# Ten weight buffers of a transformer trunk divided in another way during attention and the output projection

## The chip, the core and the metric

The kernel runs on one core of a Trainium2 chip. A core has five engines that run side by side, each with an instruction queue of its own that is worked off in order: TensorE (PE in the profile; its weight loads are listed apart as PEld), VectorE (DVE), ScalarE (ACT), GpSimd (POOL) and SyncE (SP), which here only issues DMA transfers. They share an on-chip memory of 128 partitions; matrix products land in a second one, PSUM. Engines wait for each other through semaphores. The metric is the time of one execution on the device in microseconds (us); the median of three runs before the change is 2564.08 us.

## What is computed

The reference is a stack of two layers over 1040 positions (16 learned ones and 1024 of the input) of width 1024, in float32. Each layer has two halves, each added to the residual:

```python
xn = rms_norm(h, attn_norm[i])
gq, gk, gv, gr, glr, fq, fk, fv, ff = jnp.split(xn @ w_in[i], cuts, axis=-1)
log_a = jax.nn.log_sigmoid((glr @ w_alpha_up[i] + b_alpha[i])) / GLA_TAU
o_gla = gla_chunk_causal(gq * GLA_DK ** -0.5, gk, gv, log_a)       # 4 heads, chunks of 64
o_gla = rms_norm(o_gla, gla_norm[i]) * jax.nn.silu(gr)
log_f = jax.nn.log_sigmoid((ff + b_forget[i]))
o_fox = rms_norm(forgetting_attention(fq, fk, fv, log_f), fox_norm[i])   # 8 heads, softmax
h = h + jnp.concatenate([o_gla, o_fox], axis=-1) @ w_out[i]
h = h + conv_ffn(rms_norm(h, ffn_norm[i]), w_up[i], conv_w[i], conv_b[i], w_down[i])
```

GLA is a gated linear attention with a decaying state, FoX a softmax attention with a forget bias, and `conv_ffn` an up-projection, a causal convolution of width 3, a SiLU gate and a down-projection. A last norm follows the second layer.

## The kernel before

**Activations and weights.** Activations lie transposed: eight slabs k of 128 features by 1040 positions. A weight tile m is 128 output columns of a matrix, cut into eight blocks k of 128 by 128. To keep float32 accuracy each operand is split into a rounded value ("hi", type float32r) and the remainder ("lo"), and each product is three matmuls, hi by hi, lo by hi and hi by lo: lines 225, 226 and 227, in `mm3`.

**Preparing a weight tile** (`weights`, line 174). For each half of a tile (four blocks, 128 x 512 elements, 256 KB) there are three steps: SyncE issues a DMA into a landing buffer "raw" (line 183), ScalarE rounds raw into "hi" (line 192), and VectorE, or GpSimd while `att` is set and the tile isn't one of the output projection's, subtracts hi from raw into "lo" (line 194). The buffers come from the pool "w": four for raw, three for hi and three for lo, ten of 2 KB per partition. A buffer that is asked for again waits until all that read it before have finished: raw until the cast and the subtraction are through, hi and lo until TensorE has made the last matmul with them. Callers can also hand in buffers of their own (`slots`, `keep`), and then only raw comes from the pool.

**Attention of a layer** (`attention`). `head` (line 366) computes the first three tiles; its first one is rounded by `narrow_weights`, with two hi buffers of the pool, the others lie in buffers of their own. Then come the rest of GLA and FoX. The products of a tile are work items (`add_tile`, `unit`): a tile is multiplied chunk by chunk, with three chunks of positions, and all eight blocks in each. When a tile's first chunk starts, the weights of the next tile are asked for, so that at most the running and the next tile hold buffers. These items fill TensorE between the steps of FoX (`fox`): scores, softmax, transposes, products with the values.

After the last FoX head come the first NSPLIT = 4 tiles of the output projection, summed over seven of the eight blocks in the order KORD = 4, 5, 0, 1, 2, 3, 6 and fed by VectorE's and ScalarE's splits of the mixed heads ("mh", "ml"). The last steps of FoX run among them. In attention a scheduler, which sees the whole program and an estimate of each instruction's time, sets the order on every engine, by program order among what is ready.

**The rest of the output projection** (in `ffn_up`, function `wout`, "wo" in the profile) runs twice over the eight tiles, once for each half of the positions, in an order written out by hand (`orders`). Tiles 0 to 3 have only their eighth block left, tiles 4 to 7 all eight; tiles 5 and 6 keep their weights from the first pass in other buffers (`keep`). The next tile's weights are asked for before the running tile's matmuls are issued. In the second pass VectorE and ScalarE also build the FFN's norm and its first operands ("x"); "ssq" is a small matmul that sums squares for that norm, the second one of which follows the first FFN block.

**The FFN** takes hi, lo and raw from the same pool (`block_operand`, `up_split`, from line 1003 on; rounding in lines 1042 and 1043), every second operand from a pool of its own. Its first loads and operands are asked for in `wout` at the start of the very last tile (`ensure(0)`, line 1116), five operands ahead. From the output projection on the order of TensorE's instructions is the program's.

Of the kernel before, what the change touches and what calls it, by code (L numbers as in the profile page):

```python
# [57 lines left out]
class Slots:  # L58


    def __init__(self):
        self.free = []
        self.lent = []
# [27 lines left out]
        return self.t[i]  # L91


class PsumTags:
    def __init__(self, tags):
        self.tags = tags

    def tile(self, shape, dtype, tag, name):
        pool, tag, bufs = self.tags[tag]
        return pool.tile(shape, dtype, tag=tag, name=name, bufs=bufs)  # L100
# [36 lines left out]
class Kern:  # L137
    def __init__(self, ctx, tc, hT0, wm, wd, vec, wau, out):
# [14 lines left out]
        nc.vector.memset(self.ones[:], 1.0)  # L153
        self.eps = self.vec[:, V_FIN + KD:]
        nc.vector.memset(self.eps, EPS)
        self.wp = ctx.enter_context(tc.tile_pool(name="w", bufs=3))
        self.slots = Slots()
        self.slots.add(ctx.enter_context(tc.tile_pool(name="slots", bufs=1)), NSLOT, "s")
        dp = ctx.enter_context(tc.tile_pool(name="dr", bufs=1, space=DRAM))
# [723 lines left out]
    def attention(self, lyr, nm, hsrc, chunks, feed):  # L883
        tc, nc, s = self.tc, self.nc, self.slots
        with tc.tile_pool(name=f"aps{lyr}", bufs=2, space=PSUM, reuse_waits="tile") as pp2, \
# [5 lines left out]
            with tc.tile_pool(name=f"gla{lyr}", bufs=1, reuse_waits="tile") as gp:  # L891
# [27 lines left out]
                g = [{"rem": rem}, {"rem": rem}]  # L919
                tiles = [(self.wm[lyr, M_REM], ev_rem)] + self.gla_products(lyr, 0, gp, pp, nm, g[0])  # L920
                self.head(tiles[:3], pp, nm, fd)
                if fd:
                    fd["end"]()
                add(tiles[3:])
# [121 lines left out]
    def ffn_up(self, lyr, mix, hT, pp, fw, halves, o0, during_last):  # L1046
# [14 lines left out]
        def operand(x):  # L1061
            X[x] = [[s.get(F32R, f"x{x}", (128, 2, 520)) for _ in range(2)] for _ in range(2)]
# [22 lines left out]
        def ensure(i):  # L1085
            while len(ops) < min(i + AHEAD + 1, len(seq)):
                ops.append(self.up_operand(lyr, *seq[len(ops)], fw, raws, len(ops) % 2))
# [22 lines left out]
        def wout(i, h):  # L1110
            m = orders[h][i]
            k0 = KD - 1 if m < NSPLIT else 0

            def f(w):
                if h == 1 and i == KD - 1:
                    ensure(0)
                ps = bank2("wo", (0, 1, 2, 0, 1, 3, 2, 1)[i] if h else i % 4)
                for k in range(len(w)):
                    for c in range(2):
                        self.mm3(ps[:, c, :n], w[k], mix[k0 + k], halves[h] + c * n, n, k == 0, k == len(w) - 1)  # L1120
                x = hT[m][:, sl[h]]
                nc.vector.tensor_tensor(out=two(x), in0=used(ps), in1=two(x), op=ALU.add)
                nc.gpsimd.dma_start(self.hm[m][:, sl[h]], x)
                if i == 0:
                    nc.scalar.activation(acc[:, sl[h]], x, AF.Square)
                else:
                    t = half(sq, i % 2)
                    nc.scalar.activation(t, x, AF.Square)
                    nc.vector.tensor_tensor(out=acc[:, sl[h]], in0=acc[:, sl[h]], in1=t, op=ALU.add)
                if h == 0:  # L1130
                    return
                if m < NSPLIT:
                    nc.scalar.mul(half(gt, m % 2), x, gain(m))
                else:
                    nc.vector.scalar_tensor_tensor(out=diff(m - 4), in0=x, scalar=gain(m), in1=half(gt, m % 2),
                                                   op0=ALU.mult, op1=ALU.subtract)
                if i == 1:
                    scale(0)
                    operand(1)
                    operand(2)  # L1140
                for k in turn.get(i, ()):
                    first_operand(k)
            return f
# [13 lines left out]
        for this, nxt in zip(todo, todo[1:] + [None]):  # L1157
            w, ahead = ahead, nxt and wout_weights(*nxt)
# [97 lines left out]
        for i, (j, p) in enumerate(seq):  # L1256
# [7 lines left out]
            ps, w = q[bank], ops[i]  # L1264
# [452 lines left out]
```

## Time and profile before

| what | value |
| --- | --- |
| three runs | 2564.07, 2564.08 and 2564.76 us |
| profiled execution | 2572.09 us, its span from the first to the last instruction 2570.3 us |
| mean granted TensorE clock | 0.99 |
| matmuls | 19278 |
| weight loads by DMA of 256 KB from the matrices in and up | 330 from SyncE's queue, median 2.9 us from issue to landing |

The stages, in us from the start of the span:

| stage | layer 0 | layer 1 |
| --- | --- | --- |
| attention: head, GLA | 0 to 182 | 1286 to 1450 |
| FoX | 182 to 463 | 1450 to 1730 |
| end of FoX with the first four output tiles | 463 to 531 | 1730 to 1798 |
| output projection | 531 to 585 | 1798 to 1858 |
| FFN up | 585 to 1034 | 1858 to 2309 |
| FFN down | 1034 to 1286 | 2309 to 2570 |

The profile describes one execution. Its page lists the busy time of each engine, the busy shares in 40 slices, the DMA queues, the chain of work that ended last and the costliest groups of instructions. A row of a group reads: line, engine, operation, output <- inputs, shapes, count, then busy time and mean of one, then the idle time of its engine just ahead of it with what ended it. In an order of time a row starts with the time in the span and the duration, and a bracket at its end gives the idle time ahead of it and what released it. Rows of SPq are SyncE's DMA queue. A matmul's row is longer than its share of time, since matmuls overlap.

### The profile page before, as it was taken

The page shows a single profiled execution, that of the slowest core. Times are in us where ns is not written, and L with a number is a line of the kernel's source. Part 1 is how long each engine was busy: PE and PEld are TensorE (multiplying, and loading weights), DVE is VectorE, ACT ScalarE, POOL GpSimd, SP SyncE. Part 2 cuts the span into 40 slices and gives each one's busy share as a digit, 9 for nine tenths or more (in the row PEclk, how much of TensorE's full clock was granted, in tenths as well). Part 3 has the DMA queues.
Part 4 walks back from the last instruction along what each step waited for, and adds up shares of the span by engine and source line. Part 5 has one row for each costly group of instructions (what it writes and reads, how often), then busy time and mean ns, then how long its engine had stood idle before and what let it go on. Part 6 is the DMA issues. An engine that isn't in the chain of part 4 may idle for free.

```text
span 2570.3 us, 48489 instructions
## 1 busy us (share of the span) xinstructions
PE 2496.6 (97%) x19278; PEld 2428.1 (94%) x19278; DVE 1756.6 (68%) x3394; ACT 1271.3 (49%) x2577; POOL 407.8 (16%) x582
## 2 busy tenths in 40 slices
PE   8999999999999999999999999999999999999998
PEld 7989999898999999999999899998999999999997
DVE  7655676769877777753655665676697777687435
ACT  7346666546444445641443565664464444455312
POOL 4033333210000000100301233331100000001002
PEclk9999999999999999999999999999999999999999
DMA  3232134342322224763312232152423222257712
GB/s 128 67 86 73 41 96 129 104 145 82 116 77 81 79 75 141 194 181 89 106 51 67 73 90 83 39 164 90 149 78 104 75 86 76 80 165 176 200 52 72
DMA packets 118514, 260.90 MB, mean 102 GB/s; under 512 B 14880, under 2 KB 32544, under 8 KB 118288
## 3 DMA queue, kind: packets, MB, share of 16 engines
q1 hardware_dynamic: 93984, 182.79, 22.7%
q0 software_dynamic: 22432, 72.71, 10.3%
q8 instruction: 151, 2.47, 0.4%
q10 hardware_dynamic: 1872, 2.31, 0.3%
q14 instruction: 75, 0.61, 0.1%
HBM read 177.16 MB, written 67.81 MB: 95 GB/s over the span
## 4 chain that ended last, share of the span: by engine, by line
PE 50%; issue 30%; DVE 13%; DMA 3%; ACT 3%; POOL 1%; SPq 0%; DVEq 0%; POOLq 0%; ACTq 0%
PE mm L225 8%; PE mm L226 7%; PE mm L227 7%; PE down L225 5%; PE down L227 5%; PE down L226 5%; PE av L724 2%; PE tr L706 2%; DVE P L677 2%; DVE x L1067 1%; PE S L669 1%; PE wo L226 1%; PE wo L225 1%; PE wo L227 1%; DVE cv L1217 1%
## 5 line engine op out<-in xcount | busy, mean ns | idle before, releaser
L225 PE MATMUL up<-x,hi 128*128 128x260 f32 (+1 forms) x2464 | 697.3, 283 | 2.1 <-DVE hg L1224 1.3
L227 PE MATMUL up<-x,hi 128*128 128x260 f32 (+1 forms) x2464 | 696.1, 282 | 2.3 <-DVE x L1067 2.3
L226 PE MATMUL up<-x,lo 128*128 128x260 f32 (+1 forms) x2464 | 696.4, 283 | 0.0
L227 PEld LDWEIGHTS up<-x,hi 128*128 128x128 f32 x2464 | 465.1, 189 | 3.1 <-DVE x L1067 3.1
L225 PEld LDWEIGHTS up<-x,hi 128*128 128x128 f32 x2464 | 464.8, 189 | 3.2 <-DVE hg L1224 1.7
L226 PEld LDWEIGHTS up<-x,lo 128*128 128x128 f32 x2464 | 464.6, 189 | 0.4
L1043 DVE TENSOR_TENSOR lo<-raw,hi 128x512 fp32r<-128x512 f32 x364 | 248.5, 688 | 174.4 <-ACT hi L1042 174.4
L225 PE MATMUL mm<-xh,hi 128*128 128x348 f32 (+4 forms) x1056 | 363.6, 344 | 0.0
L227 PE MATMUL mm<-xl,hi 128*128 128x348 f32 (+4 forms) x1056 | 339.9, 322 | 0.0
L226 PE MATMUL mm<-xh,lo 128*128 128x348 f32 (+4 forms) x1056 | 339.7, 322 | 0.0
L1042 ACT CAST hi<-raw 128x512 fp32r<-128x512 f32 x364 | 224.3, 620 | 145.3 <-PE up L227 84.9
L225 PEld LDWEIGHTS mm<-xh,hi 128*128 128x128 f32 x1056 | 200.2, 190 | 6.3 <-issue 5.3
L226 PEld LDWEIGHTS mm<-xh,lo 128*128 128x128 f32 x1056 | 200.3, 190 | 0.6 <-issue 0.3
L192 ACT CAST hi<-raw 128x512 fp32r<-128x512 f32 (+2 forms) x184 | 106.4, 581 | 188.9 <-PE down L227 108.9
L226 PE MATMUL down<-ah,lo 128*128 128x260 f32 (+1 forms) x704 | 198.0, 281 | 1.8 <-DVE lo L194 1.8
L227 PEld LDWEIGHTS mm<-xl,hi 128*128 128x128 f32 x1056 | 199.1, 189 | 0.6 <-issue 0.3
L227 PE MATMUL down<-al,hi 128*128 128x260 f32 (+1 forms) x704 | 198.1, 281 | 0.0
L225 PE MATMUL down<-ah,hi 128*128 128x260 f32 (+1 forms) x704 | 198.0, 281 | 0.0
L350 DVE TENSOR_TENSOR PT<-tr,PT 116x464 fp32r<-116x464 f32 (+3 forms) x240 | 122.4, 516 | 76.1 <-ACT PT L349 73.9
L685 ACT ACTIVATE P<-P,m 116x924 f32<-116x924 f32 (+4 forms) x144 | 110.4, 767 | 77.2 <-DVE m L677 71.6
L706 PE MATMUL tr<-ident,P 116*116 116x116 f32 x704 | 144.1, 269 | 1.5 <-DVE m L677 0.9
L1249 POOL DMA_DIRECT2D actd<-cv x44 | 23.6, 535 | 766.3 <-DVE cv L1248 745.4
(275 smaller groups left out, 5811.4 us busy)
## 6 DMA issues: line engine op xcount, KB each, us to landing
raw<-in_wm_dram SPq DMA_DIRECT2D x330, 256.0 KB, 2.9
raw<-in_wd_dram SPq DMA_DIRECT2D x64, 256.0 KB, 3.4
actd<-cv POOLq DMA_DIRECT2D x22, 520.0 KB, 3.0
actd<-cv POOLq DMA_DIRECT2D x22, 512.0 KB, 3.1
cb<-cd SPq DMA_DIRECT2D x16, 520.0 KB, 4.0
st<-actd SPq DMA_DIRECT2D x14, 520.0 KB, 5.4
st<-actd SPq DMA_DIRECT2D x14, 512.0 KB, 5.4
kA<-kA SPq DMA_DIRECT2D x24, 260.0 KB, 4.4
```

What stands on the lines that cost most here:

```text
L192: nc.scalar.copy(hi[:, :n, :], raw[:, :n, :])
L225: nc.tensor.matmul(ps, wh, xh[:, c0:c0 + n], start=first, stop=False, skip_group_check=more)
L226: nc.tensor.matmul(ps, wl, xh[:, c0:c0 + n], start=False, stop=False, skip_group_check=more)
L227: nc.tensor.matmul(ps, wh, xl[:, c0:c0 + n], start=False, stop=last, skip_group_check=more)
L350: nc.vector.tensor_tensor(out=lo, in0=src, in1=hi.bitcast(F32), op=ALU.subtract)
L669: nc.tensor.matmul(S[:rows, :n], q["qA"][e][:, qs], q["kA"][e][:, c0:k1], start=True, stop=False)
L677: nc.vector.tensor_tensor_reduce(out=x, in0=S[:rows, :n], in1=cb[:rows, c0:k1], scale=1.0, scalar=(BIG if ci == 0 else m[:rows, ci - 1:ci] ...
L685: nc.scalar.activation(x, x, AF.Exp, scale=-1.0, bias=low, accum_out=(den if nch < 3 else d2[:rows, 0:1]))
L706: nc.tensor.transpose(tr[:w, j, :rows], P[:rows, o:o + w], id_)
L724: nc.tensor.matmul(av[:, a:width], w.rearrange("p a b -> p (a b)"), x, start=(t == 0 and i == 0), stop=(t == last and i == 1))
L1042: nc.scalar.copy(hi[:, :nk, :], src[:, :nk, :])
L1043: nc.vector.tensor_tensor(out=lo[:, :nk, :], in0=src[:, :nk, :], in1=hi[:, :nk, :].bitcast(F32), op=ALU.subtract)
```

## The change

The pool "w" becomes ten single buffers, w0 to w9, and a class `Rings` gives them out in turn. It has two ways to divide them, chosen by a flag. With the flag off, raw has w0 to w3, lo has w4 to w6 and hi has w7 to w9: four, three and three, as before. With the flag on, raw has w0 and w1, hi has w2 to w5 and lo has w6 to w9: two, four and four. Each kind has a counter of its own in each of the two ways, which runs on through the kernel. The flag is switched on in each layer after `head` and off at the start of the last output tile of the second pass, ahead of the FFN's first requests. A buffer that changes its role waits for its last readers in the old one. No instruction is added or left out.

```diff
--- before.py
+++ after.py
@@ -89,6 +89,22 @@
 
     def __getitem__(self, i):
         return self.t[i]
+
+
+class Rings:
+
+
+    def __init__(self, pool):
+        self.pool, self.next, self.stream = pool, {}, False
+        self.tags = {"raw": range(4), "lo": range(4, 7), "hi": range(7, 10)}, \
+                    {"raw": range(2), "hi": range(2, 6), "lo": range(6, 10)}
+
+    def tile(self, shape, dtype, tag, name, bufs=None):
+        key = tag, self.stream
+        i = self.next.get(key, 0)
+        self.next[key] = i + 1
+        ids = self.tags[self.stream][tag]
+        return self.pool.tile(shape, dtype, tag=f"w{ids[i % len(ids)]}", name=name)
 
 
 class PsumTags:
@@ -153,7 +169,7 @@
         nc.vector.memset(self.ones[:], 1.0)
         self.eps = self.vec[:, V_FIN + KD:]
         nc.vector.memset(self.eps, EPS)
-        self.wp = ctx.enter_context(tc.tile_pool(name="w", bufs=3))
+        self.wp = Rings(ctx.enter_context(tc.tile_pool(name="w", bufs=1)))
         self.slots = Slots()
         self.slots.add(ctx.enter_context(tc.tile_pool(name="slots", bufs=1)), NSLOT, "s")
         dp = ctx.enter_context(tc.tile_pool(name="dr", bufs=1, space=DRAM))
@@ -919,6 +935,7 @@
                 g = [{"rem": rem}, {"rem": rem}]
                 tiles = [(self.wm[lyr, M_REM], ev_rem)] + self.gla_products(lyr, 0, gp, pp, nm, g[0])
                 self.head(tiles[:3], pp, nm, fd)
+                self.wp.stream = True
                 if fd:
                     fd["end"]()
                 add(tiles[3:])
@@ -1113,6 +1130,7 @@
 
             def f(w):
                 if h == 1 and i == KD - 1:
+                    self.wp.stream = False
                     ensure(0)
                 ps = bank2("wo", (0, 1, 2, 0, 1, 3, 2, 1)[i] if h else i % 4)
                 for k in range(len(w)):
```

## The prediction

> **What bounds the kernel now.** I read the page first, for the engine that fills the span, then the busy times by stage for where this engine idles, then TensorE's own order of time for what it waits on there.
>
> ```profile
> PE 2496.6 (97%) x19278; PEld 2428.1 (94%) x19278; DVE 1756.6 (68%) x3394; ACT 1271.3 (49%) x2577; POOL 407.8 (16%) x582
> ```
> ```profile
> 182.00:463.00 281.00, 274.39 (x1933) 263.02 (x1934) 190.39 (x591) 178.27 (x476) 102.22 (x149) 0.99 0.29 87
> 463.00:531.30 68.30, 62.33 (x393) 58.24 (x392) 44.75 (x133) 32.59 (x95) 7.81 (x17) 0.95 0.29 91
> 531.30:585.30 54.00, 53.00 (x436) 52.57 (x437) 38.03 (x65) 24.21 (x46) 9.99 (x17) 1.00 0.57 172
> ...
> 1730.30:1798.50 68.20, 61.34 (x393) 57.69 (x391) 44.40 (x133) 32.69 (x95) 7.82 (x16) 0.95 0.28 90
> ```
>
> TensorE is busy for 97% of the span, so only its idle time and its clock can give anything. A row of the second fence is a stretch: its ends and length, then the busy us (instructions) of PE, PEld, DVE, ACT and POOL, the granted clock, the DMA share and GB/s. They are, in layer 0, FoX, its end with the first four output tiles (I call it the **tail**) and the output projection; below the dots stands the tail of layer 1. TensorE idles 6.6 us in the 281 of FoX, but 6.0 and 6.9 us in some 68 in the tails, where the granted clock is also 0.95. What it waits for:
>
> ```profile
> 463.63 0.38 PE L226 MATMUL mm<-mh,lo 128*128 128x256 f32 x1 [0.27 <-DVE lo L194]
> 464.80 0.38 PE L227 MATMUL mm<-ml,hi 128*128 128x256 f32 x1 [0.78 <-DVE ml L350]
> 489.15 0.39 PE L225 MATMUL mm<-mh,hi 128*128 128x256 f32 x1 [1.92 <-ACT hi L192]
> 489.88 0.39 PE L226 MATMUL mm<-mh,lo 128*128 128x256 f32 x1 [0.23 <-DVE lo L194]
> 506.48 0.39 PE L225 MATMUL mm<-mh,hi 128*128 128x256 f32 x1 [0.31 <-ACT hi L192]
> 520.49 0.38 PE L226 MATMUL mm<-mh,lo 128*128 128x256 f32 x1 [0.15 <-DVE lo L194]
> 582.51 0.39 PE L226 MATMUL wo<-mh,lo 128*128 128x260 f32 x1 [1.00 <-DVE lo L194]
> 590.59 1.14 PE L1100 MATMUL ssq<-r,ones 128*128 128x260 f32 x4 [1.95 <-DVE r L1129]
> 1730.91 0.39 PE L226 MATMUL mm<-mh,lo 128*128 128x256 f32 x1 [0.27 <-DVE lo L194]
> 1738.18 0.39 PE L227 MATMUL mm<-ml,hi 128*128 128x256 f32 x1 [2.10 <-DVE ml L350]
> 1756.88 0.58 PE L225 MATMUL mm<-mh,hi 128*128 128x256 f32 x1 [2.05 <-ACT hi L192]
> 1773.82 0.39 PE L225 MATMUL mm<-mh,hi 128*128 128x256 f32 x1 [0.35 <-ACT hi L192]
> 1787.77 0.39 PE L226 MATMUL mm<-mh,lo 128*128 128x256 f32 x1 [0.16 <-DVE lo L194]
> 1852.96 0.58 PE L226 MATMUL wo<-mh,lo 128*128 128x258 f32 x1 [2.91 <-DVE lo L194]
> 1863.56 1.14 PE L1100 MATMUL ssq<-r,ones 128*128 128x258 f32 x4 [1.94 <-DVE r L1129]
> ```
>
> In the brackets stands TensorE's idle time and what ended it. Rows with L192 or L194 are waits for a rounded weight (hi) or its low half (lo). In GLA and in FoX before the tail TensorE had no such wait of 0.15 us or more: there the third buffer is enough.
>
> **The change part by part.** With three buffers, a tile of two halves (a with k = 0 to 3, b with k = 4 to 7) takes two, so b of the next tile must wait until a of the running one has been read for the last time. The first four output tiles run their sums in the order 4, 5, 0, 1, 2, 3, 6: a is let go just before the tile's end, and b is what the next tile needs first. That is the wait at 489.15:
>
> ```profile
> 463.33 0.61 ACT L192 CAST hi<-raw 128x512 fp32r<-128x512 f32 x1
> ...
> 488.50 0.60 ACT L192 CAST hi<-raw 128x512 fp32r<-128x512 f32 x1
> ```
> ```profile
> L194 DVE TENSOR_TENSOR lo<-raw,hi 128x512 fp32r<-128x512 f32 x100 | 68.8, 688 | 16.8 <-ACT hi L192 16.1
> ```
>
> Half a was rounded at 463.33, b only at 488.50, as the tile before ended. With four buffers both halves go into the pair of the tile before last, which TensorE has left, so b moves to about where a is now. Summed over the rows above, this removes 0.27 + 1.92 + 0.23 + 0.31 + 0.15 = 2.88 us in layer 0 and 0.27 + 2.05 + 0.35 + 0.16 = 2.83 us in layer 1: 5.7 us. No instruction is added or dropped; casts of 0.60 us and subtractions of 688 ns (on GpSimd in FoX before the tail) move earlier.
>
> The clock comes on top:
>
> ```profile
> 488.00:492.00 4.00, 2.61 (x14) 2.41 (x15) 2.81 (x7) 2.60 (x8) 0.82 (x2) 0.80 0.23 67
> 492.00:496.00 4.00, 4.00 (x26) 3.96 (x25) 1.07 (x2) 0.90 (x2) 0.00 (x0) 0.77 0.20 67
> 1754.00:1758.00 4.00, 1.95 (x11) 1.51 (x11) 3.54 (x12) 2.60 (x8) 0.43 (x1) 0.85 0.00 0
> 1758.00:1762.00 4.00, 4.00 (x26) 4.00 (x26) 1.56 (x5) 1.13 (x3) 0.43 (x1) 0.73 0.41 133
> ...
> 1854.00:1858.00 4.00, 4.00 (x20) 4.00 (x20) 3.80 (x7) 2.06 (x4) 0.35 (x1) 0.50 0.35 129
> ...
> 592.00:596.00 4.00, 4.00 (x35) 4.00 (x35) 4.00 (x7) 2.14 (x4) 0.00 (x0) 1.00 0.02 5
> ```
>
> Right after the two long waits the granted clock is below 1: 4 x (0.20 + 0.23) = 1.7 us lost in layer 0, 4 x (0.15 + 0.27) = 1.7 us in layer 1, 3.4 us together. The last row warns: after the 1.95 us at 590.59 the clock stayed at 1.00, so a gap of this length does not always cost it. The Trainium skill, "TensorE: Matmul & The Clock Gate", section "What's actually happening", says that the half clock comes after an idle window of about 3.4 us; by it, gaps of 2 us would not be the cause, the dips would stay and the sum would hold 5.7 us instead of 9.1. The trace speaks for both sides, so this is a rival below.
>
> Not all of 9.1 us need come back. While TensorE waits, the softmax chain runs on, and VectorE's rows for ml (0.78, 2.10) stay: the low halves of the mixed heads, in stretches where VectorE is the late one. Bounds are 0 and 9.1; I take off 2.0, about the longest wait on VectorE in the tail.
>
> In the **projection** three buffers also bind: the last tile's b half is rounded late, its subtraction finds VectorE full, and TensorE waits 1.00 and 2.91 us, in layer 1 with the clock at 0.50 after it (2.0 us). But the next wait, 1.95 and 1.94 us, is on VectorE itself:
>
> ```profile
> 564.00:590.50 26.50, 23.63 (x190) 22.97 (x188) 26.50 (x44) 15.87 (x28) 4.71 (x8) 1.00 0.56 178
> 1835.90:1863.50 27.60, 21.98 (x157) 21.37 (x155) 25.19 (x41) 14.95 (x27) 4.17 (x7) 0.88 0.43 134
> ```
>
> VectorE is busy for 26.5 of 26.5 us in layer 0: what TensorE gains before 590.59 it waits there. Layer 0 gives 0. In layer 1 VectorE idles 27.6 - 25.2 = 2.4 us, and no more than that comes through. Against it stands a new wait. Each layer puts 52 halves of attention's 26 tiles and 8 of each pass of the projection into the new rings, 68, a multiple of four, so the last output tile always lies in w4 and w5 (hi) and w8 and w9 (lo). The FFN's first hi is number 2 in layer 0 and number 119 in layer 1 of the old ring w7 to w9; both are w9. Its cast must now follow the last output matmul: 0.60 + 0.69 = 1.3 us with the subtraction, where before a third hi buffer was free for it. In layer 0 the 1.95 us wait covers it; without that cover it costs 1.3 us. In layer 1 it takes 1.3 of the 2.4: I count 1.0.
>
> Two **landing** buffers for four: a weight load waits on SP's queue for the subtraction two halves before, not four.
>
> ```profile
> SPq L183 <- POOL lo L194: 171.8, 20, 29.8
> ```
> ```profile
> raw<-in_wm_dram SPq DMA_DIRECT2D x330, 256.0 KB, 2.9
> ...
> raw<-in_wm_dram SPq DMA_DIRECT2D x16, 64.0 KB, 2.1
> ```
> ```profile
> DMA to landing us min/median/max: 2.5/2.9/6.1
> ```
>
> Already 171.8 us of SP's time in FoX go on that wait, with the copies of k, the decay rows and the gate's loads queued behind it. Since a pair is now rounded a tile ahead of its use (from 463.33 to 489.15 that was 26 us), a load of 2.9 us, 6.1 at worst in FoX by the last row, stays hidden there: 0. In the projection's first pass, tile m = 4 already rounded, six full and four small loads pass two buffers in 27 us, half of the stage's 54.0. Each holds its buffer for landing, cast, subtraction and, my estimate, 0.4 us of handovers, together 2.9 + 1.7 for a full and 2.1 + 1.0 for a small one: 6 x 4.6 / 2 + 4 x 3.1 / 2 = 20 us. It fits: 0.
>
> GLA and FoX get a new order of their small work; nothing there waits for weights, so 0, with 4 us to either side (a third of the 13 us that TensorE idles in FoX in two layers).
>
> **Sum.** 5.7 + 3.4 - 2.0 + 1.0 = 8.1 us. The profiled execution took 2572.09 us for a span of 2570.3; 8 us above the median of the runs, 2564.08. I take the 8.1 from the median: 2556.0 us.
>
> **The rivals.** (1) *The clock does not follow the gaps*, as the page's rule has it: 5.7 - 2.0 + 1.0 = 4.7 us, 2559.4. For it 590.59, against it four rows. (2) *The waits change their name*: the tail is held by VectorE's ml and softmax steps, and the time comes back as waits on L350 and L677. For it 464.80 and 1738.18, against it that VectorE is busy 2.8 of 4 us at the 489.15 wait. 0 to 3 us: 2563. That the change doesn't do what it says, the scheduler still placing the b casts late, would look alike and is counted here. (3) *Layer 1 gets all*: VectorE's 2.4 us and 4 us in FoX besides: 9.1 + 2.4 + 4 = 15.5 less the 2.0: 2550.6. (4) *Slower: the projection starves on two landing buffers.* At landing time L (0.7 L for a small load) its first pass needs 4.4 L + 7 us; this exceeds 27 us from L = 4.5 us. At the 6.1 us that FoX shows at worst it is 34 us, 7 us late per layer, 14 in all, less the 8 gained: 2570. For it: DMA share 0.57 there, twice that of FoX; against it the median of 2.9.
>
> **How the numbers follow.** Forecast (2556) 0.49, (1) 0.15, (2) 0.20, (3) 0.07, (4) 0.09. 0.2% is 5.1 us, about what a measurement of this kernel can tell from no change. Faster by more: forecast and (3), 0.56; within: (1) and (2), 0.35; slower: (4), 0.09. The range reaches from (3) with a little over, 2549, to 2566: forecast, (1), (2) and the milder half of the order's 4 us.
>
> **What would show it.** Right: in the tail no TensorE wait on L192 or L194, b casts next to a casts, tails under 65 us with a clock near 1; the FFN's first L1042 cast right behind the last output matmul, ssq still waiting on L1129. Wrong: landing above 4 us in the projection and casts ended by DMA (4); ml and m waits grown by what L192 lost (2); dips at unchanged places (1). A FoX stage changed by over 4 us would make the forecast wrong for a reason outside the sum.

## The result and the profile after

| | kernel before | changed kernel |
| --- | --- | --- |
| median, five runs each | 2564.76 us (2564.07 to 2571.19) | 2555.54 us (2550.99 to 2558.21) |
| six more runs beside 16 of before | 2566.91 us | 2558.23 us (2551.93 to 2561.13) |
| profiled execution, its span | 2572.09, 2570.3 us | 2556.77, 2555.0 us |

The ratio of the runs is 0.9953 with a 95% interval of 0.9943 to 0.9964, in the second set 0.9955 (0.9942 to 0.9969): faster by 0.45 to 0.47%, about 12 us by the ratios, 9 us by the medians. The two profiled executions lie 15.3 us apart, since that of before was one of its longer runs. Line numbers rise by 16 in `mm3` and `weights` and by 17 in the FFN: L208 is the cast of a weight (192 before), L210 its subtraction (194), L241 to L243 are the three matmuls (225 to 227), L1059 and L1060 the FFN's cast and subtraction (1042 and 1043).

The page of the changed kernel, part 1:

```profile
PE 2489.1 (97%) x19278; PEld 2425.4 (95%) x19278; DVE 1752.1 (69%) x3394; ACT 1272.2 (50%) x2577; POOL 409.2 (16%) x582
```

The counts are those of before. Next the busy times by stage, columns as in the prediction: first the changed kernel (FoX, tail and the stretch from the output projection's first matmul to the FFN's first gate, of layers 0 and 1), then the rows of before for that last stretch, which the prediction doesn't show.

```profile
182.90:460.60 277.70, 272.27 (x1931) 261.06 (x1929) 189.49 (x591) 177.79 (x475) 100.51 (x147) 1.00 0.29 87
...
460.60:524.10 63.50, 58.88 (x393) 57.10 (x393) 43.92 (x134) 32.26 (x94) 8.54 (x17) 0.95 0.27 90
1724.20:1786.70 62.50, 57.85 (x393) 56.21 (x393) 43.73 (x134) 31.86 (x94) 8.52 (x17) 0.97 0.27 89
524.10:628.29 104.19, 98.42 (x777) 96.41 (x777) 85.09 (x141) 52.26 (x95) 12.40 (x20) 0.97 0.43 132
1786.70:1891.01 104.31, 98.59 (x777) 96.80 (x777) 84.68 (x141) 52.33 (x95) 12.38 (x20) 0.97 0.44 132
```
```profile
531.30:632.39 101.09, 95.86 (x777) 93.97 (x777) 85.12 (x142) 52.25 (x95) 12.34 (x20) 1.00 0.42 127
1798.50:1905.14 106.64, 98.77 (x776) 97.05 (x776) 85.12 (x142) 51.85 (x95) 12.31 (x20) 0.97 0.40 121
```

In one table, with a second profile of the changed kernel (from the later set; its span is 2550.2 us). Here and below the stages are cut at marks read to 0.1 us, so that a length can be off by 0.1:

| stage, us (layer 0, layer 1) | before | after | after, second profile |
| --- | --- | --- | --- |
| FoX, up to the tail | 280.4, 279.7 | 277.7, 277.6 | 278.2, 278.3 |
| tail | 68.3, 68.2 | 63.5, 62.5 | 62.6, 62.5 |
| projection to first gate | 101.1, 106.6 | 104.2, 104.3 | 102.5, 104.0 |
| all the rest | 1666.0 | 1665.2 | 1662.1 |

The tails give 10.5 us (11.4 in the second profile). The stretch behind them loses 3.1 us in layer 0 (1.4) and gains 2.3 in layer 1 (2.6), so together it gives nothing or little. FoX gives 4.8 us (3.6), which the sum hadn't.

What TensorE waits for now in the tails and at the start of the FFN, from its order of time:

```profile
464.15 0.39 PE L243 MATMUL mm<-ml,hi 128*128 128x256 f32 x1 [0.65 <-DVE ml L366]
468.14 0.58 PE L243 MATMUL mm<-ml,hi 128*128 128x256 f32 x1 [2.96 <-DVE ml L366]
579.27 0.58 PE L241 MATMUL up<-x,hi 128*128 128x260 f32 x1 [2.36 <-ACT hi L1059]
580.58 0.59 PE L242 MATMUL up<-x,lo 128*128 128x260 f32 x1 [0.73 <-DVE lo L1060]
1727.72 0.39 PE L243 MATMUL mm<-ml,hi 128*128 128x256 f32 x1 [0.64 <-DVE ml L366]
1731.72 0.38 PE L243 MATMUL mm<-ml,hi 128*128 128x256 f32 x1 [2.96 <-DVE ml L366]
1842.45 0.58 PE L241 MATMUL up<-x,hi 128*128 128x258 f32 x1 [2.66 <-ACT hi L1059]
1843.54 0.58 PE L242 MATMUL up<-x,lo 128*128 128x258 f32 x1 [0.51 <-DVE lo L1060]
```

No wait on L208 or L210 is left in the tails. A wait of 2.96 us on ml stands in each, where before stood 0.53 and 2.10 us at the same matmul. At the FFN's start TensorE waits for the first cast and its subtraction; the waits for the sum of squares (1.95 and 1.94 us) are gone. ScalarE's order of time in layer 0 ends with that cast:

```profile
576.92 0.64 ACT L1146 ACTIVATE sq<-h 128x520 f32<-128x520 f32 x1 [1.54 <-DVE h L1140]
...
578.60 0.61 ACT L1059 CAST hi<-raw 128x512 fp32r<-128x512 f32 x1
```

The last output matmul ended at 579.27 - 2.36 = 576.91. The cast had to follow it, and it stands behind three other rows of ScalarE as well, of which the first is shown, and starts 1.7 us later.

The clock at the two places that the prediction had dips at (same columns):

```profile
488.00:492.00 4.00, 3.75 (x29) 3.51 (x28) 3.19 (x9) 2.02 (x7) 0.42 (x1) 1.00 0.46 133
492.00:496.00 4.00, 4.00 (x27) 3.96 (x26) 2.03 (x7) 2.27 (x7) 0.86 (x2) 1.00 0.00 0
1756.00:1760.00 4.00, 4.00 (x28) 3.92 (x27) 1.24 (x4) 1.16 (x5) 0.43 (x1) 1.00 0.00 0
1760.00:1764.00 4.00, 4.00 (x32) 3.96 (x31) 2.60 (x12) 2.73 (x10) 0.00 (x0) 1.00 0.00 0
```

Both are at 1.00. Behind the wait on ml, in layer 0, it is not:

```profile
468.00:472.00 4.00, 3.86 (x14) 3.52 (x14) 4.00 (x11) 2.98 (x9) 1.52 (x3) 0.50 0.24 60
```

Cut at their own ends, the dips in the traces stand at 0.50 for 3.41 us (490.42 to 493.83 in the kernel before) or for twice that. A tail had two of 3.41 us before. Now layer 1 has one, behind the wait on ml, and layer 0 has one of 6.8 us there, so that its mean clock is 0.95 as before. In the second profile each tail has one of 3.41 us (mean clock 0.97). ScalarE and VectorE, in order of time, show how the second tile's weights are prepared:

```profile
459.84 0.63 ACT L208 CAST hi<-raw 128x512 fp32r<-128x512 f32 x1
...
460.98 0.61 ACT L208 CAST hi<-raw 128x512 fp32r<-128x512 f32 x1
```
```profile
462.40 1.28 DVE L210 TENSOR_TENSOR lo<-raw,hi 128x512 fp32r<-128x512 f32 x2
...
467.67 2.29 DVE L366 TENSOR_TENSOR ml<-h,mh 128x256 fp32r<-128x256 f32 x5
```

Halves a and b are now cast 1.1 us apart, not 25. Their two subtractions, 1.28 us, run on VectorE ahead of the low halves (ml) for which TensorE then waits.

### The profile page after: what moved, and what is told of

It is laid out like the page before. It is cut to its first block, busy times and chain, and to the rows that moved or that the text cites. A ratio compares the mean times of both kernels' runs of the same rounds, so it can differ in the third digit from the quotient of the medians.

```text
span 2555.0 us, 48526 instructions
## 1 busy us (share of the span) xinstructions
PE 2489.1 (97%) x19278; PEld 2425.4 (95%) x19278; DVE 1752.1 (69%) x3394; ACT 1272.2 (50%) x2577; POOL 409.2 (16%) x582
## 4 chain that ended last, share of the span: by engine, by line
PE 51%; issue 31%; DVE 10%; DMA 3%; ACT 3%; POOL 1%; SPq 0%; DVEq 0%; POOLq 0%; ACTq 0%
PE mm L241 8%; PE mm L243 7%; PE mm L242 7%; PE down L241 5%; PE down L242 5%; PE down L243 5%; PE av L740 3%; PE tr L722 2%; DVE P L693 1%; DVE x L1084 1%; PE wo L241 1%; PE wo L243 1%; PE wo L242 1%; PE S L685 1%; PE S L686 1%
## 5 line engine op out<-in xcount | busy, mean ns | idle before, releaser
L241 PE MATMUL up<-x,hi 128*128 128x260 f32 (+1 forms) x2464 | 699.8, 284 | 8.2 <-ACT hi L1059 5.0
L243 PE MATMUL up<-x,hi 128*128 128x260 f32 (+1 forms) x2464 | 698.1, 283 | 2.1 <-DVE x L1084 2.1
L241 PEld LDWEIGHTS up<-x,hi 128*128 128x128 f32 x2464 | 466.7, 189 | 10.2 <-ACT hi L1059 5.4
L243 PEld LDWEIGHTS up<-x,hi 128*128 128x128 f32 x2464 | 467.2, 190 | 2.9 <-DVE x L1084 2.9
L1060 DVE TENSOR_TENSOR lo<-raw,hi 128x512 fp32r<-128x512 f32 x364 | 248.0, 686 | 172.9 <-ACT hi L1059 172.8
L241 PE MATMUL mm<-xh,hi 128*128 128x348 f32 (+4 forms) x1056 | 362.8, 344 | 0.0
L243 PE MATMUL mm<-xl,hi 128*128 128x348 f32 (+4 forms) x1056 | 339.6, 322 | 0.0
L1059 ACT CAST hi<-raw 128x512 fp32r<-128x512 f32 x364 | 224.2, 620 | 145.9 <-PE up L243 84.9
L241 PEld LDWEIGHTS mm<-xh,hi 128*128 128x128 f32 x1056 | 199.7, 189 | 6.3 <-issue 5.3
L208 ACT CAST hi<-raw 128x512 fp32r<-128x512 f32 (+2 forms) x184 | 106.5, 581 | 190.2 <-PE down L243 116.2
L243 PEld LDWEIGHTS mm<-xl,hi 128*128 128x128 f32 x1056 | 198.5, 188 | 1.0 <-issue 0.7
L243 PE MATMUL down<-al,hi 128*128 128x260 f32 (+1 forms) x704 | 198.1, 281 | 0.0
L241 PE MATMUL down<-ah,hi 128*128 128x260 f32 (+1 forms) x704 | 198.0, 281 | 0.0
L366 DVE TENSOR_TENSOR PT<-tr,PT 116x464 fp32r<-116x464 f32 (+3 forms) x240 | 122.5, 516 | 70.8 <-ACT PT L365 68.2
```

The costliest lines, as they stand in the source:

```text
L208: nc.scalar.copy(hi[:, :n, :], raw[:, :n, :])
L241: nc.tensor.matmul(ps, wh, xh[:, c0:c0 + n], start=first, stop=False, skip_group_check=more)
L243: nc.tensor.matmul(ps, wh, xl[:, c0:c0 + n], start=False, stop=last, skip_group_check=more)
L366: nc.vector.tensor_tensor(out=lo, in0=src, in1=hi.bitcast(F32), op=ALU.subtract)
L1059: nc.scalar.copy(hi[:, :nk, :], src[:, :nk, :])
L1060: nc.vector.tensor_tensor(out=lo[:, :nk, :], in0=src[:, :nk, :], in1=hi[:, :nk, :].bitcast(F32), op=ALU.subtract)
```

## The experiments

The kernels ran in three sets, each beside runs of the kernel before on the same chip (medians 2566.12, 2567.17 and 2566.91 us). The theory, called PAIRS below: the gain is the wait for a fourth pair of rounded and low buffers in the tails; landing in two buffers is free; and where the buffers change their role something is given back. The rivals are named in the expectations. Line numbers of the experiments differ from those of the changed kernel by a few.

| kernel | median, us | ratio to before (95%) | FoX, us | tail, us | projection to gate, us |
| --- | --- | --- | --- | --- | --- |
| new division in GLA and FoX only | 2564.47 | 0.9989 (0.9979 to 0.9999) | 279.0, 278.0 | 68.4, 67.8 | 101.1, 106.6 |
| in the tail only | 2569.17 | 1.0012 (1.0004 to 1.0021) | 287.7, 281.7 | 63.1, 64.7 | 102.6, 105.4 |
| in the projection only | 2575.52 | 1.0028 (1.0017 to 1.0039) | 279.2, 277.7 | 68.7, 68.4 | 105.5, 109.7 |
| two for landing, three pairs | 2572.82 | 1.0020 (1.0008 to 1.0032) | 281.0, 278.0 | 68.9, 68.2 | 104.0, 106.6 |
| before, natural order of blocks | 2562.56 | 0.9975 (0.9965 to 0.9985) | 283.0, 278.7 | 63.6, 64.1 | 101.1, 106.1 |
| that, and a later request | 2558.19 | 0.9957 (0.9944 to 0.9969) | 280.4, 278.9 | 63.2, 63.2 | 102.6, 105.8 |
| changed, other buffers at the FFN | 2555.09 | 0.9953 (0.9939 to 0.9967) | 280.2, 277.8 | 63.3, 63.2 | 102.0, 104.1 |
| changed, later request | 2553.47 | 0.9944 (0.9932 to 0.9957) | 279.9, 276.9 | 62.1, 62.6 | 103.2, 104.9 |
| changed, both | 2552.89 | 0.9945 (0.9932 to 0.9958) | 280.5, 276.7 | 62.7, 62.0 | 104.6, 103.8 |

**1. Only in GLA and FoX.** The flag goes off again just ahead of the first output weights, and stays off.

```diff
+                        self.wp.stream = False
                         ready = self.weights(self.wm[lyr, M_WO], vec=True)
```

> The new division of the ten buffers only in the GLA and FoX sweeps; it goes back to four, three and three just ahead of the first output weights, so the output tiles have the buffers of before. Theory PAIRS (the gain comes from four pairs of rounded and low weights in the output tiles beside the end of FoX, and in layer 1's projection; what FoX gained in the profiled run, 2.7 and 2.1 us, is another order of the same work): the tails stay 68 us, the projections 54 and 59.6, FoX moves by at most 3 us a layer; time 2559 to 2565 (before: 2564.8). Rival REORDER (an earlier release in the GLA and FoX sweeps gives the gain): FoX 277.6 in both layers and 2556 to 2559. Rival LUCK (the gain is clock dips that fall differently from run to run): within 2 us of before here and in all four kernels of this set.

Tails and projections are those of before to within 0.5 us. The whole gains 0.1%, hardly apart from nothing, and within PAIRS' range. REORDER falls; LUCK falls with the kernels that follow, which lie up to 9 us above before. FoX takes 279.0 and 278.0 us; but the third kernel of the table, whose FoX has the buffers of before, has 279.2 and 277.7. What FoX seemed to gain is no more than two profiles of the same FoX differ by. A gain of a microsecond a layer isn't ruled out: FoX takes 279.2 to 283.0 and 277.7 to 279.7 us with the old division (before, experiments 3, 5 and 6) and 277.7 to 280.5 and 276.7 to 278.3 with the new one (both profiles of the changed kernel, experiments 1 and 7 to 9).

**2. Only in the tail.**

```diff
+                        self.wp.stream = True
                         ready = self.weights(self.wm[lyr, M_WO], vec=True)
...
+        self.wp.stream = False
         ahead = wout_weights(*todo[0])
```

> The new division only from the first output weights to the end of attention; the projection and all before the tail have four, three and three. PAIRS: tails 63 to 64 us in both layers (before 68.3 and 68.2), no wait of TensorE on a weight's rounding there, but a wait of some 3 us on the activations' low halves at the second chunk; the projections as before or longer; the FFN's first rounding as before, so that the stretch from there to the first gate stays 47.0 us; time 2552 to 2557, under or near the changed kernel. REORDER: tails 68, time as before. LUCK: within 2 us of before.

The tails give 5.2 and 3.5 us, as PAIRS has it, though not without waits on weights: 2.13 and 1.71 us on a first low half (L210). And yet the kernel is slower than before: FoX ahead of the tails costs 7.3 and 2.0 us more. The order of time around the switch in layer 0, queue of SyncE, GpSimd, ScalarE, and then the busy times with the clock:

```profile
421.94 0.33 SPq L199 DMA_DIRECT2D raw<-in_wm_dram  x1
```
```profile
419.55 0.44 POOL L858 TENSOR_TENSOR cb<-cb,mask 116x116 f32<-116x116 f32 x1 [3.81 <-DMA cb<-cd]
420.04 0.56 POOL L968 DMA_DIRECT2D h<-mixd  x1
420.62 1.30 POOL L210 TENSOR_TENSOR lo<-raw,hi 128x512 fp32r<-128x512 f32 x1
```
```profile
425.70 0.62 ACT L208 CAST hi<-raw 128x512 fp32r<-128x512 f32 x1 [7.35 <-DMA raw<-in_wm_dram]
```
```profile
424.00:428.00 4.00, 1.63 (x12) 1.37 (x10) 0.22 (x2) 2.30 (x8) 0.54 (x1) 0.97 0.42 134
428.00:432.00 4.00, 1.07 (x4) 0.90 (x5) 3.96 (x14) 3.59 (x12) 0.42 (x1) 0.50 0.08 31
```

Read it from the top: the load is issued at 421.94, as a subtraction on GpSimd ends at 420.62 + 1.30 = 421.92. It is the subtraction of the load two before; with four landing buffers a load waits for the one four before. That subtraction stood behind a mask step that waited 3.81 us for a DMA. The load lands 3.7 us later. ScalarE works its queue off in order and stands 7.35 us ahead of the cast, and TensorE, which needs ScalarE's softmax, is busy 1.63 and 1.07 of 4 us with the clock down to 0.50. The changed kernel has two landing buffers here too, but its weights are rounded earlier: there the subtraction two loads before has ended at 402.4, and the load is issued at 406.98. So it is the place of the switch that costs more than the pairs bring, by a wait for a landing buffer and not for one that changes its role.

**3. Only in the projection.**

```diff
+        self.wp.stream = True
         ahead = wout_weights(*todo[0])
```

> The new division only in the output projection of each layer, from its first weights to the FFN. PAIRS: tails 68 us as before, projection of layer 1 some 56 us in place of 59.6, of layer 0 54 to 55 us; the FFN's first rounding lands on a buffer that the last output matmuls still read, so TensorE waits 2.4 to 2.7 us for it and the stretch to the first gate grows from 47.0 to 48.6 or 49.0; net 2562 to 2567, no gain or little. REORDER: as before. A theory by which the projection is the main gain (rival PROJECTION): 2557 to 2560.

No gain: 0.28% slower, outside the expected 2562 to 2567 too. The projection itself takes 52.7 and 57.2 us in place of 54.1 and 59.5, but the stretch from the FFN's first matmul to the gate 52.8 and 52.5 in place of 47.0. TensorE's order of time, layer 0:

```profile
585.51 0.58 PE L242 MATMUL up<-x,lo 128*128 128x260 f32 x1 [2.03 <-DVE lo L1059]
592.03 1.79 PE L1116 MATMUL ssq<-r,ones 128*128 128x260 f32 x4 [1.95 <-DVE r L1146]
```

Here the wait for the sum of squares stays, and a wait on the FFN's first low half comes on top. PROJECTION falls: no gain comes through here.

**4. Two for landing, but three pairs.**

```diff
-                    {"raw": range(2), "hi": range(2, 6), "lo": range(6, 10)}
+                    {"raw": range(2), "hi": range(7, 10), "lo": range(4, 7)}
```

> The changed kernel, but with two buffers for landing and only three for rounded and three for low halves while the new division is on (the other two lie idle). Theory PAIRS: the two landing buffers cost nothing by themselves, and without a fourth pair the gain goes: tails 67 to 69 us with the waits on weights back, layer 1's projection 58 to 60 us, 2563 to 2569. A theory by which fewer landing buffers order the DMAs better, or by which the gain lies in where the buffers lie (rival LANDING): 2554 to 2560. If two landing buffers cost (rival STARVED): over 2572, with TensorE in the projection waiting on rounding that waits on a DMA.

The gain is gone, and the waits of the tail are back where they were, in TensorE's order of time:

```profile
490.78 0.39 PE L241 MATMUL mm<-mh,hi 128*128 128x256 f32 x1 [2.02 <-ACT hi L208]
...
1758.06 0.38 PE L241 MATMUL mm<-mh,hi 128*128 128x256 f32 x1 [1.91 <-ACT hi L208]
```

LANDING falls. PAIRS holds for the tails; the time lies above its 2563 to 2569 and in the range of STARVED, whose sign is there too, in layer 0: the projection takes 57.7 us against 54.1, with TensorE waiting 1.05, 0.34 and 0.58 us for weights around 561 to 566, and the cast that ended the first of these waits had itself waited 3.14 us for its load. So beside four pairs TensorE has no such wait with two landing buffers, and beside three it has.

**5. The buffers of before, another order.** In tiles 1 to 3 the blocks run from 0 to 6, so half a, which is asked for first, is needed first, and is let go four blocks sooner.

```diff
-                            self.add_tile(w, pp, self.wm[lyr, M_WO + m], mix, chunks[::-1], ev, ks=KORD, vec=True, **first)
+                            self.add_tile(w, pp, self.wm[lyr, M_WO + m], mix, chunks[::-1], ev, ks=range(KD - 1) if m else KORD, vec=True, **first)
```

> The kernel before with its buffers as they were; only the order of the seven row blocks in output tiles 1 to 3 beside the end of FoX is 0 to 6 in place of 4, 5, 0, 1, 2, 3, 6. The second four blocks' buffers are then first used four blocks later, and the first four blocks' are free four blocks sooner. PAIRS, as a matter of release times: three pairs are then enough, the waits on weights (2.88 and 2.83 us) go as in the changed kernel and the tails are 63 to 65 us, with no collision at the FFN's start; time 2553 to 2559. If four pairs as such are needed (rival COUNT): tails 67 to 69 us and 2563 to 2566. LUCK: within 2 us of before.

COUNT falls: with three pairs the waits on L192 in the tails go from 2.23 and 2.40 us to 0 and 0.20 (0.6 us on L194 stays in each layer), and the tails take 63.6 and 64.1 us. The place of the old dip:

```profile
486.00:490.00 4.00, 4.00 (x31) 3.80 (x30) 2.52 (x11) 2.26 (x7) 0.43 (x1) 1.00 0.52 204
490.00:494.00 4.00, 3.57 (x28) 3.15 (x28) 3.74 (x12) 2.56 (x7) 0.44 (x1) 1.00 0.03 4
```

The clock stays at 1.00 there, and the gain of 0.25% has an interval clear of 1, but it is only about half of the changed kernel's. The median lies 3.6 us above PAIRS' upper end; the profiled run shows FoX at 283.0 us in layer 0, whose code is that of before.

**6. That, and the second tile's weights asked for one chunk later.**

```diff
-        if not box.get("ahead"):
+        if not box.get("ahead") and not (feed and c0 == CH[2][0]):
```

> The kernel before, its buffers as they were, with the natural order of blocks in output tiles 1 to 3 and the later request of the second tile's weights: the two edits that free the tail without any change of buffers. PAIRS as a matter of release times: tails 62 to 64 us as in the changed kernel, projections 54 and 59.5 as before, FFN's start 47 as before; 2556 to 2561. COUNT (four pairs are needed): 2563 or more. If the FFN's start and layer 1's projection cancel in the changed kernel, the two are within 3 us of each other.

2558.19 us, beside 2558.23 us of the changed kernel in the same set: the ratios are 0.9957 and 0.9955. The time is inside PAIRS' range, and COUNT falls by it as well. Two edits without any new division of the buffers give what the change gives, as far as these runs can tell. The tails of this kernel:

```profile
461.40:524.60 63.20, 59.76 (x394) 56.75 (x393) 44.74 (x135) 32.65 (x96) 8.03 (x17) 0.97 0.31 100
1724.20:1787.40 63.20, 59.48 (x394) 56.39 (x393) 44.71 (x135) 32.60 (x95) 8.00 (x17) 0.97 0.30 102
```

**7. The changed kernel, other first buffers for the FFN.** When the old division comes back, its counters are set so that the first rounded block goes to w7 and its low half to w6.

```diff
                     self.wp.stream = False
+                    self.wp.turn()
...
+    def turn(self):
+        for tag, i in (("raw", 2), ("hi", 0), ("lo", 2)):
+            self.next[tag, False] = i
```

> The changed kernel, with the first buffers of the old division chosen anew where it comes back ahead of the FFN: the first rounded block goes to a buffer that the last but one output tile has left, not to the one that the last output matmuls read. Theory COLLISION (one buffer with two parts costs the 2.36 + 0.73 and 2.66 + 0.51 us of TensorE's waits at the FFN's start, and the slow clock behind them): those waits go, a wait of at most 2 us for the sum of squares comes back, the stretch from the FFN's first matmul to its first gate is 46 to 47.5 us in place of 49.0 and 48.6; 2550 to 2554 us (changed kernel: 2555.5). Rival FULL (VectorE is what arrives last there, and the wait only changes its name): from the projection's first matmul to the gate 104 us as in the changed kernel, 2554 to 2557.

The waits on the FFN's first cast go, as COLLISION has it (0.51 and 0.82 us on its low half remain), and the rest is as FULL has it: to the gate it takes 49.4 and 51.1 us, where COLLISION has 46 to 47.5. The time, 2555.09 us, lies in FULL's range, 1 us above COLLISION's, which alone would not separate them. TensorE's order of time, and the busy times from the FFN's first matmul to the gate:

```profile
584.67 1.15 PE L1121 MATMUL ssq<-r,ones 128*128 128x260 f32 x4 [3.18 <-DVE r L1152]
...
1844.87 1.14 PE L1121 MATMUL ssq<-r,ones 128*128 128x258 f32 x4 [3.10 <-DVE r L1152]
```
```profile
577.70:627.10 49.40, 43.08 (x343) 41.38 (x341) 49.40 (x82) 29.18 (x53) 2.65 (x4) 1.00 0.26 77
1837.50:1888.60 51.10, 44.67 (x342) 43.11 (x341) 49.78 (x82) 29.76 (x54) 2.86 (x4) 0.97 0.26 75
```

VectorE is busy 49.40 of 49.40 us in layer 0 and 49.78 of 51.10 in layer 1. The projection is 2.6 us shorter than in the changed kernel, and the wait for the sum of squares is back, with 3.2 us in place of the 1.95 of before.

**8. The changed kernel, the later request** (the edit of 6 alone).

> The changed kernel, with the second output tile's weights asked for in the second chunk of the first tile in place of the first, so that their two subtractions (1.28 us on VectorE) stand behind the low halves of the second chunk. Theory ORDER (the wait of 2.96 us on low halves grew because these subtractions now come ahead of them): that wait falls to some 1.7 us or less and the dip of the clock behind it shrinks, tails 60 to 62.5 us; 2551 to 2555. Rival FULL (VectorE has more than it can do there whatever the order): tails 63 to 64 us with the wait later, 2554 to 2557.

ORDER holds for the wait it named: none on ml is left. But 1.72 us on the softmax maximum and 1.20 us on a transposed probability stand there now in each layer, in layer 0's order of time:

```profile
468.43 0.47 PE L685 MATMUL S<-kA,qA 128*116 128x460 f32 x1 [1.72 <-DVE m L693]
...
474.10 1.05 PE L740 MATMUL av<-PT,V 112*128 112x232 f32 x7 [1.20 <-DVE PT L366]
```

These are VectorE's as well. The tails are 62.1 and 62.6 us, at the upper end of ORDER's range; the time is 2553.47, inside it, 2 us under the changed kernel, with intervals that overlap.

**9. Both edits.**

> Both edits, the choice of buffers at the FFN's start and the later request of the second tile's weights. COLLISION and ORDER together: 2547 to 2552. FULL: 2553 to 2557.

2552.89 us lies between the two ranges, 0.1 us under FULL's. It is the lowest median of the study and the interval of its ratio, 0.9932 to 0.9958, overlaps that of the changed kernel, so that it beats the changed kernel isn't shown.

**10. Both, and work moved from VectorE to GpSimd.** In the second pass of the projection GpSimd makes the low halves of the weights and five of the seven additions to the sum of squares.

```diff
+                    eng = nc.gpsimd if h == 1 and i < 6 else nc.vector
-                    nc.vector.tensor_tensor(out=acc[:, sl[h]], in0=acc[:, sl[h]], in1=t, op=ALU.add)
+                    eng.tensor_tensor(out=acc[:, sl[h]], in0=acc[:, sl[h]], in1=t, op=ALU.add)
...
-            w = self.weights(self.wm[lyr, M_WO + m][:, KD - 1 if m < NSPLIT else 0:KD, :], keep=keep.get(m))
+            w = self.weights(self.wm[lyr, M_WO + m][:, KD - 1 if m < NSPLIT else 0:KD, :], keep=keep.get(m), pool=h == 1)
```

> The kernel with both edits (choice of buffers, later request), and beside them, in the second half of each output projection, the subtractions of the weights and the running sum of squares of the second to sixth tile on GpSimd in place of VectorE. Theory FULL (from the second half of the projection to the first gate VectorE is busy all the time: 49.9 of 51.2 us behind the projection, so that TensorE's 3.2 us wait for the sum of squares is VectorE's backlog): this takes some 5 us of VectorE off that stretch and layer; from the projection's first matmul to the gate 100 to 102 us in place of 104 and 104, 2545 to 2551. Rival CHAIN (the sum of squares is late by its own chain, ScalarE's squares and the last additions; GpSimd's 1.3 us additions make the chain longer): 103 to 106 us, 2552 to 2558.

2564.59 us, ratio 0.9988 (0.9978 to 0.9998): worse than both theories. The projection takes 57.2 and 58.3 us, where the kernel with both edits has 53.3 and 52.9, and the gate's first addition on VectorE comes 106.4 and 106.6 us behind the projection's first matmul against 103.8 and 103.0. TensorE in layer 0:

```profile
580.38 0.38 PE L245 MATMUL up<-x,hi 128*128 128x260 f32 x1 [2.96 <-ACT hi L1063]
582.88 0.59 PE L246 MATMUL up<-x,lo 128*128 128x260 f32 x1 [2.12 <-DVE lo L1064]
```

The FFN's first operand is late again. CHAIN is nearer, but its place was the sum of squares, and TensorE doesn't wait there in layer 0. FULL wasn't put to the test: up to the gate VectorE has 13 rows fewer in layer 0 (126 for 139), and yet it is busy 84.1 us where the kernel with both edits has 84.5. Rows of it grew while GpSimd ran beside them, two in layer 0 above all:

```profile
560.43 3.66 DVE L307 SCALAR_TENSOR_TENSOR nt<-nt 128x520 f32<-128x520 f32 x1 [2.43 <-ACT nt L306]
...
571.85 2.83 DVE L1127 SCALAR_TENSOR_TENSOR h<-h,vec,r 128x520 f32<-128x520 f32 x1
```

These rows take 0.69 and 0.75 us in the kernel with both edits. Which of the two moves costs wasn't separated.

**11. Both, and the sum of squares' product later.**

```diff
-        before = {1: second_half, 2: make_t2, 7: make_t3, 8: make_n4, 10: make_t1, 12: make_b22}
+        before = {3: second_half, 4: make_t2, 7: make_t3, 8: make_n4, 10: make_t1, 12: make_b22}
```

> The kernel with both edits; the product with ones for the second half's sum of squares stands behind three of the FFN's products in place of one, and what needs it behind four. FULL: TensorE's 3.2 us wait goes, and comes back as waits for the operands a little later, since VectorE is as late as before: from the projection's first matmul to the gate 102.5 to 105 us, 2550 to 2555. Rival CHAIN (only this one chain is late, VectorE has room behind it): 99.5 to 101.5 us, 2545 to 2549.

2559.37 us (ratio 0.9961, 0.9949 to 0.9973). The 3.2 us wait goes, and waits of 0.2 to 1.1 us for the operands x come in its place up to the gate, whose first addition comes 105.0 and 105.8 us behind the projection's first matmul (the mark of the table lies 0.8 us later). CHAIN falls; FULL had the kind right, the stretch 1 us and the time 4 us too low.

**12. The changed kernel once more.**

> The changed kernel once more, beside the others of this set: 2551 to 2558 by its own earlier runs; ratio 0.994 to 0.9965.

2558.23 us and a ratio of 0.9955: the ratio is as expected, the median 0.2 us above the range. The stages of this second profile stand in the table of the section on the result; what else it adds is the last section's.

## Why the prediction was right

2556.0 us was predicted, 2555.54 measured, and 2558.23 in the second set. That the first two agree to 0.5 us is luck: the 8.1 us were taken off a median of three runs, 2564.08, and the later sets put the kernel before at 2566.1 to 2567.2. By the ratios the gain is some 12 us. The mechanism and most of the signs were right, the sum a third too small. Most of what it lacked is in the tails, for which it had 7.1 us and which give 10.5: TensorE's idle time there fell by 3.6 us, from 12.8 to 9.3, much as the sum had it (5.7 less 2.0), but its busy time by 6.9 where the sum had 3.4. Step by step:

**Waits on weights in the tails, 5.7 us.** Right, and shown from two sides: they return with three pairs (2.02 and 1.91 us, experiment 4), and without a fourth pair they fall to 0.6 and 0.8 us when the order lets the buffers go sooner (experiment 5). So the mechanism was the release time, as the prediction had it, and the number of buffers is one way to it.

**Clock behind them, 3.4 us.** Right in kind: behind the long wait on a cast (1.9 to 2.1 us) the clock falls in all eight tails that have it (before, experiments 1, 3 and 4), and at this place it stays at 1.00 in the tails of every other run, which rules out rival 1 in the form "the dips stay". The size, net, was half of that in the first profile, since the wait on ml now has its own dips: at 1.7 us for 3.41 us of half clock the two tails lost 6.8 us before, 5.1 after, and 3.4 in the second profile. So the clock gave 1.7 us back, or 3.4. TensorE's busy time, though, fell from 62.33 + 61.34 to 58.88 + 57.85 us for the same 393 instructions each. A second part of this, which the sum put at nothing, are the waits themselves: the row ahead of a wait isn't overlapped by the next and counts with its full 0.38 us (463.63 in the prediction's rows), where rows of its size in an unbroken run start 0.12 us apart (490.10, 490.22, 490.34 in the same trace). Waits of 0.14 us or more went from 18 to 8, which by this makes some 2.5 us, an estimate. What the remaining 2 to 3 us are isn't settled.

**Less 2.0 for what does not come back.** Right in size, which is partly luck, since the 2.0 was the longest wait there and not the growth of one. TensorE's waits on ml were 0.78 + 0.40 + 0.53 us before in layer 0 and 0.78 + 0.39 + 2.10 in layer 1; they are 0.65 + 2.96 and 0.64 + 2.96 now: 2.2 us more. The reason was narrower than "the late engine": the second tile's two subtractions come ahead of the low halves. Asking later removes this wait and brings 2.9 us of others on the same engine (experiment 8), so rival 2, a changed name, is true of this one part of the tail.

**Projection, 0 and 1.0.** The sum was right within 2 us, its parts were not. In layer 0 the cover held in its number: 0.76 + 1.00 + 1.95 = 3.71 us of waits before, 0.76 + 2.36 + 0.73 = 3.85 after, and yet the stretch is 3.1 us longer, since the clock fell to 0.50 behind the new wait (TensorE's busy time is 98.42 us against 95.86). The price of the new wait, 1.3 us, was mis-sized: it came to 3.1 and 3.2 us, because the cast starts not with the end of the last output matmul but 1.7 us behind it (576.91 to 578.60), after other rows of ScalarE. In layer 1, 2.3 to 2.6 us came through, where the step let 2.4 through and took 1.3 off. That VectorE is the end there is what experiment 7 speaks for, where TensorE's wait only changes its name, and experiment 11; the direct test, experiment 10, did not relieve VectorE and so leaves it open.

**"ssq still waiting on L1129"**, said of the FFN's start, was wrong for the first profile: the wait on the cast took its place. In the second a wait of 0.77 us on it is there in layer 0.

**Two landing buffers, 0.** In the changed kernel TensorE has no wait for it, though ScalarE's casts in the projection now do end on DMAs, a sign that the prediction had put down for rival 4. Beside three pairs it costs (experiment 4). The 0 held, with less room than the estimate of 20 of 27 us suggested: in the first pass loads of 256 KB land in 3.6 and 3.5 us (median of each layer), not 2.9, which in rival 4's formula makes 4.4 x 3.6 + 7 = 23 us.

**FoX, 0 with 4 us to either side.** It fell by 2.7 and 2.1 us in the profile, and 279.2 and 277.7 us with the old buffers (experiment 3) show that this is within what profiles of the same work differ by.

The price of the switch is what the prediction saw least of. It named one place, the FFN's start, and set it too low; that the place is a choice which can cost 9 us (FoX in experiment 2) it did not consider.

## What to carry to other kernels

Where an engine waits for a rotating buffer, look at which half is let go last and which is needed first before buying another buffer: running the blocks in the order in which the halves are asked for, and asking later, gave here what four pairs gave. Where a division of buffers switches, the last reader of each buffer is a new wait for whoever writes it next, and in an in-order queue all that stands behind that writer waits too (7.35 us of ScalarE in experiment 2): choose a place where that reader is long done, and look at every engine behind it. And where another engine is busy all the time (VectorE, 49.40 of 49.40 us), removing one of TensorE's waits lets the next one grow.

## What the hardware showed that was not expected

The same gap in the same program can cost the clock or not. First the changed kernel's two profiles at the FFN's start, TensorE's waits 2.36 + 0.73 us in the one (above) and 2.23 + 0.92 us in the other. In the first profile the clock fell:

```profile
580.00:584.00 4.00, 3.42 (x16) 3.42 (x17) 4.00 (x7) 1.23 (x2) 0.54 (x1) 0.50 0.25 91
```

In the second it did not:

```profile
578.49 0.39 PE L241 MATMUL up<-x,hi 128*128 128x260 f32 x1 [2.23 <-ACT hi L1059]
579.80 0.39 PE L242 MATMUL up<-x,lo 128*128 128x260 f32 x1 [0.92 <-DVE lo L1060]
```
```profile
578.00:582.00 4.00, 2.59 (x19) 2.39 (x20) 4.00 (x7) 0.78 (x2) 0.15 (x1) 1.00 0.03 10
582.00:586.00 4.00, 3.23 (x24) 2.91 (x23) 4.00 (x8) 3.30 (x7) 0.39 (x1) 1.00 0.39 136
```

TensorE's busy time up to the gate is 98.42 us in the one and 95.92 in the other, 2.5 us for a dip of 6.8. In experiment 7 the gap of 3.18 us in layer 0 left the clock at 1.00, and the one of 3.10 us in layer 1 of the same run did not:

```profile
1844.00:1848.00 4.00, 3.13 (x16) 3.02 (x17) 4.00 (x8) 2.55 (x5) 0.54 (x1) 0.79 0.25 97
```

Gaps of some 2.0 us in the tails (489 and 1757 before) cost it eight times out of eight. The length of a gap alone doesn't tell. What a dip costs is steadier: but for those that reach the end of a run, all in these traces stand at 0.50 for 3.41 or 6.83 us, which costs TensorE up to 1.7 or 3.4 us of work. So a stage's time in a single profile can be off by that much.

The Trainium skill, "TensorE: Matmul & The Clock Gate", section "What's actually happening", says that activity is watched in a free-running window of about 3.4 us, so that the same kernel can differ from run to run (it says so of a kernel's start). These profiles agree with that, and the 3.41 us with the window's length; that the half clock needs a whole idle window of this length does not agree with the 2.0 us gaps.
